# Three groups of small transfers move from SyncE's DMA queue to GpSimd's, in a backbone layer pair with chunked delta-rule heads

## The chip, the cores and the metric

The kernel runs on one core of one Trainium2 chip. The metric is the device time of one execution in microseconds. The engines are named as in the profile: PE (TensorE matmuls), PEld (its weight loads), DVE (VectorE), ACT (ScalarE), POOL (GpSimd) and SP (SyncE, which only issues DMAs here). A DMA can be issued from SP, from ACT or from POOL; each of the three has a queue of its own, and a wait in front of an issue holds everything behind it on that engine.

## The reference

The reference is a two-layer backbone over 256 latent tokens and 256 context tokens, all in float32, with a width of 2048. Layer 0 joins gated delta-rule heads (run in both directions over chunks of 64 tokens) with neighbourhood-attention heads. Layer 1 is a gated short convolution. Each layer has a SwiGLU block of hidden width 5632. The part that the change touches is the delta rule, and in it the inverse of a triangular matrix for each chunk, head and direction:

```python
m = jnp.where(i[:, None] > i[None, :], jnp.einsum('bhnid,bhnjd->bhnij', kb, k) * decay, 0.0)
t_inv = lax.linalg.triangular_solve(eye + m, eye, left_side=True, lower=True, unit_diagonal=True)
u = t_inv @ (v * beta);  w = t_inv @ (kb * exp(gc))
# scan over the chunks, with state S, for each direction
v_new = u_c - w_c @ S
o_c   = qd_c @ S + a_c @ v_new              # latent tokens only
S     = S * exp(gl_c) + kd_c.T @ v_new
```

The scan runs first over the context, from a zero state, and then over the latent tokens from the state that the context leaves. The context gives no output of its own.

## The kernel before, in words

**The main stream.** The time is filled with large matrix products. Weights come from HBM in tiles of 128 x 1024 floats (`raw`, 4 buffers, issued on SP at L235). ACT rounds each to float32r (`whi`, L175) and DVE takes the remainder (`wlo`, L249), with 3 buffers of each. PE then makes three products for each pair of inputs (hi x hi, hi x lo, lo x hi), at L302, L303, L307 and L319 where tokens are the output's partitions, and at L347 where features are. Beside it an adaptive-norm job streams `ada_w` through DVE (`araw`, issued at L435, used at L441).

**The order.** The program is written as generators that are interleaved by hand; a list of steps (`plan`, with the constants `P_CH` and `P_INV`) says at which step of the main stream the delta-rule parts are written. The scheduler of the framework then orders each engine's instructions once, from a simulated timeline and by the program's order as priority. On the chip each engine works through its list in order.

**The delta rule.** It is done for the context (`seq` = 1) and then for the latent tokens (`seq` = 0), in two groups of four heads (`q`).

- `chunk_matrices(seq)` builds the matrices `nt` (L994, DVE) block by block, for 2 x 2 pairs of `q` and token half. Their 32-wide off-diagonal blocks are copied by POOL into `n32` (L1013), the 64-wide ones by ACT into `n64` (L1015), the diagonal blocks into `dgs`. `nt` has one buffer. `n64` and `n32` are stored to HBM (L1020, L1021) and `dgs` too (L1023). The diagonal blocks come back in another layout as `lsol`, are inverted on DVE in 31 steps of forward substitution (L1036, L1038), and the inverses and their transposes are stored as `dz` (L1045: 4 DMAs, two out of `lsol`).
- `load_diag(dz, q)` clears two tiles with POOL, `xd` (L1060) and `xdT` (L1061), and loads the inverses' diagonal blocks into them: 8 DMAs on SP (L1066), each of 32 rows with 16 runs of 128 bytes. It is called four times, so there are 32 such DMAs. `xd` lies in one room (`diag`, or `kT` for the last call); `xdT` has two buffers, so its loads can be issued one call ahead.
- `inverses(off, diag, q)` completes the inverse from blocks of 32 to 64 and to 128, with small matmuls (L1092, L1099, L1105).
- `scan(q, seq, ...)` runs the recurrence with matmuls (L1130, L1139, L1150, L1158, L1172), DVE (L1133, L1163, L1174) and ACT (L1154). It loads keys (`ktok`, L956) and values (`vtok`, L956). For the context's second group the keys lie in the room of `lsol`.
- All of these parts take their PSUM banks from one pool of two (`gd`), in the order of the program: first inverse, second inverse, the two context scans, the latent tokens' two inverses, the two latent scans. The names in the code are `own_chunks`, `first_inverse`, `second_inverse`, `first_own` and `latents`.

**What runs meanwhile on the main stream.** Keys and values of the attention heads (`kb_d`, `vb_d`, staged through `nst`, 3 buffers, copied out of PSUM at L170 and L172 and stored on SP at L1260), then the queries, for which the context's half of the input is dropped and the latent half is loaded again as `hC`, with 7 DMAs of 512 KB on POOL (L1284). Then the attention itself (with `kb`, `vb` and `br` loaded on SP), the gate, and the output projection. The projection takes the attention's features first and the delta rule's (`yhi`, `ylo`) last.

The program reserves a scratch for the descriptors of POOL's DMAs: `dynamic_dma_scratch_size=1024` (L1702), in bytes of each partition.

Of the kernel before, what the change touches and what calls it, by code (L numbers as in the profile page):

```python
# [111 lines left out]
def body(tc, x, c, ctx, c_ctx, ada_w, ada_b, norm_mix, norm_ffn, ffn_w_gate, ffn_w_up, ffn_w_down,  # L112
# [3 lines left out]
    PE, ACT, DVE, POOL, SP = nc.tensor, nc.scalar, nc.vector, nc.gpsimd, nc.sync  # L116
# [43 lines left out]
    def smt():  # L160
        small.append(small.pop(0))
        return small[0].tile([128, 512], F32, name="sm", tag="sm")
# [11 lines left out]
    def acopy(dst, src):  # L174
        ACT.activation(dst, src, AF.Copy)  # L175
# [367 lines left out]
    def gdt():  # L543
        return gdp.tile([128, 512], F32, name="gd", tag="gd")
# [18 lines left out]
    p = smt()  # L563
# [114 lines left out]
    kd = dram.tile([128, 4, 8, 128], F32, name="kd")  # L678
# [5 lines left out]
    def hslice(d_, t0, n, q):  # L684
        return d_[:, t0:t0 + n, q * 4:q * 4 + 4, :].rearrange("p t h e -> p t (h e)")
# [125 lines left out]
    for b in range(8):  # L811
# [4 lines left out]
        p = smt()  # L816
# [119 lines left out]
    def g4(name, tag, bufs=1):  # L936
        return gw.tile([128, 1024], F32, name=name, tag=tag, bufs=bufs)

    def g2(name, bufs=G2):
        return gw.tile([128, 4, 128], F32, name=name, tag="m2", bufs=bufs)  # L940
# [10 lines left out]
        ACT.activation(em, pD.rearrange("p (i e) -> p i e", i=4), AF.Exp)  # L951
        return em

    def load_tok(tag, d_, t0, q, room=None):
        t = (g4(tag, tag) if room is None else room).rearrange("p (t h e) -> p t h e", t=2, h=4)
        SP.dma_start(t.rearrange("p t h e -> p t (h e)"), hslice(d_, t0, 2, q))  # L956
        return t

    def load_feat(tag, src, pool_=None, bufs=1):
        t = (pool_ or gw).tile([128, 1024], F32, name=tag, tag=tag, bufs=bufs).rearrange("p (h t) -> p h t", h=4)  # L960
        SP.dma_start(t, src)
        return t

    def chunk_matrices(seq):


        t0 = 2 * seq
        if seq:
            n64 = gw.tile([128, 16, 64], F32, name="n64", tag="n64", bufs=1)
            n32 = gw.tile([128, 16, 32], F32, name="n32", tag="n32", bufs=1)  # L970
            dgs = g4("dgs", "diag")
        else:
            n64 = lgo.tile([128, 1024], F32, name="n64", tag="o_t", bufs=2).rearrange("p (n c) -> p n c", n=16)
            n32 = g4("n32", "vtok")[:, 0:512].rearrange("p (n c) -> p n c", n=16)
            dgs = lgo.tile([128, 1024], F32, name="dgs", tag="o_t", bufs=2)
        dgs = dgs.rearrange("p (n c) -> p n c", n=32)
        for q in range(2):
            ktok = load_tok("ktok", kd, t0, q)
# [6 lines left out]
            for ti in range(2):  # L985
# [25 lines left out]
                for j in range(4):  # L1011
                    d, i = j % 2, j ^ 1
# [4 lines left out]
        lsol = g4("lsol", "lsol").rearrange("p (r c) -> p r c", r=32)  # L1017
        nd64 = dram.tile([128, 16, 64], F32, name="nd64", tag="nd64", bufs=2)
        nd32 = dram.tile([128, 16, 32], F32, name="nd32", tag="nd32", bufs=2)
        SP.dma_start(nd64, n64)  # L1020
        SP.dma_start(nd32, n32)  # L1021
        dl = dram.tile([4, 32, 32, 32], F32, name="dl", tag="dl", bufs=2)
        SP.dma_start(dl.rearrange("b r n c -> (b r) n c"), dgs)  # L1023
        for b in range(4):
# [16 lines left out]
        dz = dram.tile([2, 4, 2, 2, 8, 1024], F32, name="dz", tag="dz", bufs=2)  # L1041
# [14 lines left out]
    def load_diag(dz, q, tag="diag"):  # L1056

        xd = g4("xd", tag).rearrange("p (n c) -> p n c", n=16)
        xdT = gw.tile([128, 16, 128], F32, name="xdT", tag="xdT", bufs=XDT)
        POOL.memset(xd, 0.0)  # L1060
        POOL.memset(xdT, 0.0)  # L1061
        for b in range(4):
            s_ = slice(b * 32, b * 32 + 32)
            c_ = slice((b % 2) * 32, (b % 2) * 32 + 32)
            for v, m_ in ((0, xd[s_, :, c_]), (1, xdT[s_, :, s_])):
                SP.dma_start(m_, dz[v, b, q].rearrange("d t (r c) -> r (d t) c", r=32))  # L1066
        return xd, xdT

    def inverses(off, diag, q):
# [42 lines left out]
    def scan(q, seq, xdT, AT=None, qT=None, kT=None, o_t=None):  # L1112

        hs = [q * 4 + i for i in range(4)]
        if kT is None:
            kT = load_feat("kT", kTd[:, seq, q * 4:q * 4 + 4, :])
        ktok = load_tok("lsol" if seq and q else "ktok", kd, 2 * seq, q)
        vtok = load_tok("vtok", vd_, 2 * seq, q, lgo.tile([128, 1024], F32, name="vtok1", tag="o_t", bufs=2) if seq and q else None)
        visited = set()
        for step in range(2):  # L1120
            for d in range(2):
                ti = step if d == 0 else 1 - step
                tt = 2 * seq + ti
                tok = slice(ti * 128, ti * 128 + 128)
                zero = seq and step == 0
                sv = state[:, d, q * 4:q * 4 + 4, :]
                if not zero:
                    pP = gdt()
                    for i in range(4):
                        PE.matmul(pP[:, i * 128:(i + 1) * 128], kT[:, i, tok], sv[:, i, :], start=True, stop=True)  # L1130
                    R = g2("R")
                    for i in range(4):
                        DVE.scalar_tensor_tensor(R[:, i, :], pP[:, i * 128:(i + 1) * 128],  # L1133
                                                 negegc[:, d, tt, hs[i]:hs[i] + 1], vtok[:, ti, i, :],
                                                 op0=OP.mult, op1=OP.add)
                if not seq:
                    pQ = gdt()
                    for i in range(4):
                        PE.matmul(pQ[:, i * 128:(i + 1) * 128], qT[:, i, tok], sv[:, i, :], start=True, stop=True)  # L1139
                    for i in range(4):  # L1140
                        o = o_t[:, ti, i, :]
                        e = eg[:, 0, d, tt, hs[i]:hs[i] + 1]
                        if tt in visited:
                            DVE.scalar_tensor_tensor(o, pQ[:, i * 128:(i + 1) * 128], e, o, op0=OP.mult, op1=OP.add)
                        else:
                            ACT.activation(o, pQ[:, i * 128:(i + 1) * 128], AF.Copy, scale=e)
                pY = gdt()
                for i in range(4):
                    rhs = vtok[:, ti, i, :] if zero else R[:, i, :]
                    PE.matmul(pY[:, i * 128:(i + 1) * 128], xdT[:, d * 8 + ti * 4 + i, :], rhs, start=True, stop=True)  # L1150
                if seq or step == 0:
                    vd = g2("vd")
                    for i in range(4):
                        ACT.activation(vd[:, i, :], pY[:, i * 128:(i + 1) * 128], AF.Copy,  # L1154
                                       scale=brest[:, d, tt, hs[i]:hs[i] + 1])
                    pS = gdt()
                    for i in range(4):
                        PE.matmul(pS[:, i * 128:(i + 1) * 128], ktok[:, ti, i, :], vd[:, i, :], start=True, stop=True)  # L1158
                    if zero:
                        acopy(sv, pS.rearrange("p (i e) -> p i e", i=4))  # L1160
                    else:
                        for i in range(4):
                            DVE.scalar_tensor_tensor(sv[:, i, :], sv[:, i, :], eg[:, 2, d, tt, hs[i]:hs[i] + 1],  # L1163
                                                     pS[:, i * 128:(i + 1) * 128], op0=OP.mult, op1=OP.add)
                if not seq:
                    vn = g2("vn")
                    for i in range(4):
                        ACT.activation(vn[:, i, :], pY[:, i * 128:(i + 1) * 128], AF.Copy,
                                       scale=beta[:, d, tt, hs[i]:hs[i] + 1])
                    pA = gdt()  # L1170
                    for i in range(4):
                        PE.matmul(pA[:, i * 128:(i + 1) * 128], AT[:, d * 8 + ti * 4 + i, :], vn[:, i, :], start=True, stop=True)  # L1172
                    ov = o_t[:, ti]
                    DVE.tensor_tensor(ov, ov, pA.rearrange("p (i e) -> p i e", i=4), op=OP.add)  # L1174
                visited.add(tt)

    ATs = []
    parts = chunk_matrices(1)

    for q in range(2):  # L1180
# [40 lines left out]
    def own_chunks():  # L1221
        nonlocal off, diag, own
        own = chunk_matrices(0)
        off = load_offdiag(parts)
        diag = load_diag(parts[2], 0)

    def first_inverse():
        nonlocal diag
        xdTs.append(inverses(off, diag, 0))
        diag = load_diag(parts[2], 1)  # L1230

    def second_inverse():
        nonlocal off, diag
        xdTs.append(inverses(off, diag, 1))
        for q in range(2):
            scan(q, 1, xdTs[q])
        xdTs.clear()
        off = load_offdiag(own)
        diag = [load_diag(own[2], q, ("diag", "kT")[q]) for q in range(2)]
# [176 lines left out]
    def norm_row(t):  # L1416

        DVE.tensor_reduce(ss2[:, t:t + 1], ssx[:, t, :], axis=AX.X, op=OP.add)
        return rstd(rpool, ss2[:, t:t + 1], [128, 1], 1, D, f"nx{t}")
# [222 lines left out]
    for half in range(2):  # L1642
# [8 lines left out]
        for f in range(8):  # L1651
            k = half * 8 + f
            p = smt()
# [25 lines left out]
    for t in range(2):  # L1679
        r = norm_row(t)  # L1680
        for n in range(2):
            for m in range(2):
                v = xs[:, t, (2 * n + m) * 512:(2 * n + m + 1) * 512]
# [34 lines left out]
```

## Time and profile before

| What | Value |
|---|---|
| median of three runs | 2697.98 us (2696.09 to 2699.02) |
| the profiled execution | 2700.74 us |
| its span | 2698.6 us |
| PE busy | 2646.0 us, 98% of the span |
| DVE busy | 1915.9 us, 71% |
| ACT busy | 1274.9 us, 47% |
| POOL busy | 47.8 us, 2% |
| mean DMA rate | 253 GB/s |

The difference of 2.1 us between time and span lies outside the program's own instructions. The delta-rule parts lie between 230 and 785 us of the span; everything after that is feed-forward, the short convolution and their weights. Matmuls overlap in the records (one of 512 columns follows another after 0.227 us, though each is shown with 0.39), so a busy PE is not read as a PE at its peak; an idle one is a stop. In the timelines a row has its start, its length, engine, line and tiles, and in brackets the idle time of the engine before it and what ended that. A group of waits shows the sum, the number and the longest. SPq stands for SP's queue.

### The profile page before, as it was taken

The numbers are of one execution on the slowest core, as the hardware profiler recorded it, in microseconds if no ns is written. First come the engines' busy times: TensorE is split into PE (matmuls) and PEld (weight loads), VectorE is DVE, ScalarE is ACT, GpSimd is POOL, SyncE is SP. The second block draws the span as 40 slices with busy tenths as digits, with TensorE's granted clock in tenths as the row PEclk, the third lists the DMA queues.
The fourth block names the chain that finished last, engine by engine and source line by source line (L and its number), as shares of the span: only waits on it lengthen the run. The fifth ranks groups of instructions, "written<-read, shape, count | busy, mean of one in ns | idle before, by whom it ended". The sixth has DMA issues, their size and how long they took to land.

```text
span 2698.6 us, 37488 instructions
## 1 busy us (share of the span) xinstructions
PE 2646.0 (98%) x13775; PEld 2183.0 (81%) x13775; DVE 1915.9 (71%) x2645; ACT 1274.9 (47%) x1848; POOL 47.8 (2%) x73
## 2 busy tenths in 40 slices
PE   6999999999999999999999999999999999999998
PEld 4688888888887888888888878888788888888886
DVE  3378798866698866776788878898565655545665
ACT  3258633235455444444455564444454444445554
POOL 0000101010000000000000000000000000000000
PEclk8999999999999999999999999999999999999999
DMA  9945588996496988888887859997576777666653
GB/s 368 357 150 172 182 267 262 295 306 188 158 348 239 330 290 293 291 288 291 277 294 261 298 180 331 334 338 255 167 254 220 238 228 237 209 202 212 194 195 110
DMA packets 280027, 682.02 MB, mean 253 GB/s; under 512 B 50813, under 2 KB 93461, under 8 KB 278435
## 3 DMA queue, kind: packets, MB, share of 16 engines
q1 hardware_dynamic: 273516, 666.46, 73.5%
q10 hardware_dynamic: 4423, 9.50, 1.0%
q0 software_dynamic: 1904, 3.67, 0.4%
q8 instruction: 108, 1.77, 0.3%
q14 instruction: 76, 0.62, 0.1%
HBM read 657.48 MB, written 22.05 MB: 252 GB/s over the span
## 4 chain that ended last, share of the span: by engine, by line
PE 90%; DVE 3%; DMA 3%; ACT 1%; SPq 1%; issue 1%; DVEq 0%; ACTq 0%
PE mm L302 21%; PE mm L307 21%; PE mm L303 21%; PE mm L347 10%; PE mm L319 8%; PE sm L194 2%; PE sm L605 1%; PE gd L347 1%; DMA araw<-in_ada_w_dram 1%; DMA dz<-lsol 1%; DVE acc L441 1%; PE sm L1328 0%; PE gd L949 0%; DMA xn<-in_ctx_dram 0%; DVE wlo L249 0%
## 5 line engine op out<-in xcount | busy, mean ns | idle before, releaser
L249 DVE TENSOR_TENSOR wlo<-raw,whi 128x1024 fp32r<-128x1024 f32 x800 | 971.9, 1222 | 458.6 <-ACT whi L175 450.0
L175 ACT ACTIVATE whi<-raw 128x1024 fp32r<-128x1024 f32 x800 | 843.9, 1062 | 844.1 <-PE mm L307 627.8
L302 PE MATMUL mm<-whi,fhi 128*128 128x512 f32 x1232 | 482.0, 393 | 2.6 <-DVE fhi L1475 2.6
L303 PE MATMUL mm<-wlo,fhi 128*128 128x512 f32 x1232 | 479.7, 390 | 0.5 <-DVE wlo L249 0.5
L307 PE MATMUL mm<-whi,flo 128*128 128x512 f32 x1232 | 389.9, 390 | 0.0
L407 DVE SCALAR_TENSOR_TENSOR acc<-araw,cT,acc 128x1024 f32<-128x1024 f32 x224 | 286.7, 1280 | 39.8 <-DMA araw<-in_ada_w_dram 36.9
L302 PEld LDWEIGHTS mm<-whi,fhi 128*128 128x128 f32 x1232 | 231.3, 188 | 50.9 <-DVE fhi L1475 4.0
L307 PEld LDWEIGHTS mm<-whi,flo 128*128 128x128 f32 x1232 | 231.1, 188 | 48.4
L303 PEld LDWEIGHTS mm<-wlo,fhi 128*128 128x128 f32 x1232 | 231.2, 188 | 47.7 <-DVE wlo L249 1.2
L302 PE MATMUL mm<-whi,ahi 128*128 128x512 f32 x664 | 259.0, 390 | 0.0
L303 PE MATMUL mm<-wlo,ahi 128*128 128x512 f32 x664 | 258.3, 389 | 0.0
L347 PE MATMUL mm<-hB,whi 128*128 128x512 f32 (+1 forms) x840 | 234.6, 366 | 1.0 <-DVE hB L629 1.0
L307 PE MATMUL mm<-whi,alo 128*128 128x512 f32 x664 | 206.6, 389 | 0.0
L347 PEld LDWEIGHTS mm<-hB,whi 128*128 128x128 f32 x840 | 147.7, 189 | 24.5 <-DVE hB L629 2.3
L178 ACT ACTIVATE ahi<-prodT 128x256 fp32r<-128x256 f32 x176 | 73.0, 418 | 182.9 <-PE mm L303 178.0
L347 PE MATMUL mm<-hB,wlo 128*128 128x512 f32 (+1 forms) x420 | 149.7, 365 | 0.0
L307 PEld LDWEIGHTS mm<-whi,alo 128*128 128x128 f32 x664 | 124.6, 188 | 26.0
L302 PEld LDWEIGHTS mm<-whi,ahi 128*128 128x128 f32 x664 | 124.7, 188 | 25.7
L303 PEld LDWEIGHTS mm<-wlo,ahi 128*128 128x128 f32 x664 | 124.6, 188 | 25.6
L441 DVE SCALAR_TENSOR_TENSOR acc<-araw,cT,acc 128x512 f32<-128x512 f32 x180 | 133.9, 746 | 2.9 <-DMA araw<-in_ada_w_dram 2.3
L302 PE MATMUL mm<-whi,dhi 128*128 128x512 f32 x336 | 131.1, 392 | 1.2 <-DVE dhi L1475 1.2
L303 PE MATMUL mm<-wlo,dhi 128*128 128x512 f32 x336 | 130.7, 390 | 0.0
(412 smaller groups left out, 3523.3 us busy)
## 6 DMA issues: line engine op xcount, KB each, us to landing
araw<-in_ada_w_dram SPq DMA_DIRECT2D x288, 512.0 KB, 5.3
raw<-in_ffn_w_down_dram SPq DMA_DIRECT2D x176, 512.0 KB, 4.7
raw<-in_ffn_w_gate_dram SPq DMA_DIRECT2D x160, 512.0 KB, 4.4
raw<-in_ffn_w_up_dram SPq DMA_DIRECT2D x160, 512.0 KB, 4.7
raw<-in_ev_w_in_dram SPq DMA_DIRECT2D x112, 512.0 KB, 4.2
araw<-in_ada_w_dram SPq DMA_DIRECT2D x192, 256.0 KB, 5.1
raw<-in_od_w_in_dram SPq DMA_DIRECT2D x96, 512.0 KB, 5.1
raw<-in_ev_w_out_dram SPq DMA_DIRECT2D x32, 512.0 KB, 7.0
```

The lines of the kernel that those rows point to most:

```text
L175: ACT.activation(dst, src, AF.Copy)
L178: ACT.activation(hi, src, AF.Copy)
L194: return PE.transpose(dst, src, ident[:n, :n])
L249: last_lo[0] = DVE.tensor_tensor(lo, raw, hi, op=OP.subtract).ins
L302: PE.matmul(ps[ti][n], a, hi[:, n * 512:(n + 1) * 512], start=first, stop=False)
L303: ins = PE.matmul(ps[ti][n], a, lo[:, n * 512:(n + 1) * 512], start=False, stop=False).ins
L307: last_mm[0] = PE.matmul(ps[ti][n], b, hi[:, n * 512:(n + 1) * 512], start=False, stop=False).ins
L319: ins = PE.matmul(ps[ti][n], a(t), w[:, c_], start=False, stop=a is ll and hi is group[-1][0]).ins
L347: last_mm[0] = PE.matmul(o, wt, h_(slice(0, len(ws)), mv, k), start=i == 0 and g == 0 and j == 0, stop=i == len(ks) - 1 and g == len(group ...
L407: DVE.scalar_tensor_tensor(acc, raw, cT[:, k:k + 1], acc, op0=OP.mult, op1=OP.add)
L441: DVE.scalar_tensor_tensor(accs[n], raws.pop(i), cT[:, k:k + 1], accs[n], op0=OP.mult, op1=OP.add)
L605: ins = PE.matmul(pr[32 * j:32 * j + 32, :], cT2[:, g + j, :], raw[:, j].rearrange("p s n -> p (s n)"), start=g == 0, stop=g == KT - 4).ins
```

## The change

Three groups of DMAs are issued from POOL instead of SP: the store of `n32` (L1021, 2 DMAs of 256 KB), the loads of the inverse's diagonal blocks (L1066, 32 DMAs of 64 KB), and the load of the context's second keys (the call of `load_tok` in `scan` with `seq` and `q` both 1, 1 DMA of 512 KB). Nothing is added or taken away; sizes, sources, targets and tiles stay as they are.

```diff
-    def load_tok(tag, d_, t0, q, room=None):
+    def load_tok(tag, d_, t0, q, room=None, queue=SP):
         t = (g4(tag, tag) if room is None else room).rearrange("p (t h e) -> p t h e", t=2, h=4)
-        SP.dma_start(t.rearrange("p t h e -> p t (h e)"), hslice(d_, t0, 2, q))
+        queue.dma_start(t.rearrange("p t h e -> p t (h e)"), hslice(d_, t0, 2, q))
         return t
...
         SP.dma_start(nd64, n64)
-        SP.dma_start(nd32, n32)
+        POOL.dma_start(nd32, n32)
...
             for v, m_ in ((0, xd[s_, :, c_]), (1, xdT[s_, :, s_])):
-                SP.dma_start(m_, dz[v, b, q].rearrange("d t (r c) -> r (d t) c", r=32))
+                POOL.dma_start(m_, dz[v, b, q].rearrange("d t (r c) -> r (d t) c", r=32))
...
-        ktok = load_tok("lsol" if seq and q else "ktok", kd, 2 * seq, q)
+        ktok = load_tok("lsol", kd, 2 * seq, q, queue=POOL) if seq and q else load_tok("ktok", kd, 2 * seq, q)
```

## The prediction

> **What bounds the kernel now.** I read the page first, then PE's waits in the stretch that the edit touches (380 to 780 us), then the windows around the one long wait, and last the queue of SP and the timelines of POOL, DVE and ACT there.
>
> ```profile
> span 2698.6 us, 37488 instructions
> ...
> PE 2646.0 (98%) x13775; PEld 2183.0 (81%) x13775; DVE 1915.9 (71%) x2645; ACT 1274.9 (47%) x1848; POOL 47.8 (2%) x73
> ...
> PE 90%; DVE 3%; DMA 3%; ACT 1%; SPq 1%; issue 1%; DVEq 0%; ACTq 0%
> ```
>
> PE is the bound. A DMA that leaves SP earlier is worth only the PE time that is now lost waiting. PE's waits from 380 to 780 us:
>
> ```profile
> PE mm L347 <- DVE nst L172: 3.4, 1, 3.4
> PE gd L1130 <- DMA kT<-kTd: 1.0, 1, 1.0
> PE mm L347 <- issue: 0.6, 1, 0.6
> ```
>
> So 5.0 us of visible idle, most of it one wait. The windows from there on (PE's busy time and matmuls first, granted clock, DMA share and GB/s last):
>
> ```profile
> 564.00:568.00 4.00, 0.63 (x5) 0.63 (x6) 1.35 (x2) 0.71 (x3) 1.39 (x1) 1.00 0.72 200
> 568.00:572.00 4.00, 4.00 (x24) 4.00 (x23) 3.01 (x4) 2.11 (x2) 0.00 (x0) 0.57 0.98 250
> 572.00:576.00 4.00, 4.00 (x36) 4.00 (x36) 2.65 (x7) 2.09 (x5) 0.00 (x0) 1.00 1.03 375
> ```
>
> The wait costs more than its idle: in the 4 us after it the granted clock is 0.57 and PE runs 24 matmuls, where the next 4 us have 36. That is 4 x (1 - 24/36) = 1.3 us by count and 4 x 0.43 = 1.7 by clock; I take 1.5. The wait is worth 3.4 + 1.5 = 4.9 us. Where does it come from? From SP's queue, whose own waits between 380 and 700 us include:
>
> ```profile
> SPq L956 <- DMA dz<-lsol: 8.9, 1, 8.9
> ...
> SPq L1021 <- POOL n L1013: 5.9, 1, 5.9
> ...
> SPq L1020 <- ACT n L175: 0.8, 1, 0.8
> ```
>
> ```profile
> 547.64 0.33 SPq L435 DMA_DIRECT2D araw<-in_ada_w_dram  x1
> 557.00 0.38 SPq L956 DMA_DIRECT2D lsol<-kd  x1
> ...
> 561.15 3.62 SPq L1260 DMA_DIRECT2D vb_d<-nst  x3
> ```
>
> ```profile
> 552.96 0.69 DVE L172 COPY nst<-mm 128x512 f32<-128x512 f32 x1 [1.59 <-PE mm L319]
> ...
> 566.62 0.69 DVE L172 COPY nst<-mm 128x512 f32<-128x512 f32 x1 [6.10 <-DMA vb_d<-nst]
> ```
>
> The load of the second keys (L956, into the room lsol) waits until the stores of dz have read lsol, and SP is in order: from 548.0 to 557.0 nothing leaves it. Behind it stand the stores of the values. The last source that DVE wrote was begun at 552.96, yet they leave from 561.15 on. So the next copy into nst finds no free buffer until 566.62, the PSUM bank stays taken, and PE stops.
>
> **The change, part by part.**
>
> *The second keys' load, 1 DMA of 512 KB, L956 to POOL.* SP no longer stands from 548.0 to 557.0. With the dz loads gone too, the value stores follow when their data is there, about 555 instead of 561.15. They land 4.2 us after issue, about 559, before DVE asks for the buffer at 566.62 - 6.10 = 560.5. Gain 4.9 us of PE. On POOL the load stands in the same wait, behind the last hC load and ahead of the memset of xdT that POOL then waits to do, so nothing new is late. PE reads it first at 577.01:
>
> ```profile
> 577.01 1.06 PE L1158 MATMUL gd<-vd,lsol 128*128 128x128 f32 x8
> ```
>
> ```profile
> vb_d<-nst SPq DMA_DIRECT2D x8, 256.0 KB, 4.2
> ```
>
> *The store of n32, 2 DMAs of 256 KB, to POOL.* It stands behind the copies that fill n32 on the same engine, so it waits for nothing. SP's 5.9 us go, but the store of n64 is next on SP and left only 1.2 us after it, released by ACT's copy of n64 (the wait of 0.8 above). SP would stand there instead.
>
> ```profile
> 471.24 0.33 SPq L1021 DMA_DIRECT2D nd<-n  x1
> 472.46 0.33 SPq L1020 DMA_DIRECT2D nd<-n  x1
> ```
>
> PE lost nothing there before. I cost it at 0, between -1.2 and 0.
>
> *The 32 loads of the diagonal blocks, 64 KB each, to POOL.* SP's own 0.3 to 0.5 us per issue were hidden. The price lies on POOL:
>
> ```profile
> 501.28 0.96 POOL L1060 MEMSET xd<- 128x1024 f32 x1 [23.23 <-PE gd L1092]
> ...
> 529.28 2.26 POOL L1284 DMA_DIRECT2D hC<-h_d  x3 [2.21 <-PE mm L307]
> 538.73 0.72 POOL L1284 DMA_DIRECT2D hC<-h_d  x1 [7.19 <-issue]
> 541.44 1.36 POOL L1284 DMA_DIRECT2D hC<-h_d  x1 [1.98 <-issue]
> ...
> 593.17 0.95 POOL L1060 MEMSET xd<- 128x1024 f32 x1 [27.79 <-DMA raw<-in_ev_w_in_dram]
> 599.43 1.82 POOL L1061 MEMSET xdT<- 128x2048 f32 x1 [5.31 <-PE gd L1150]
> ```
>
> ```profile
> DMA to landing us min/median/max: 7.8/10.1/13.0
> ```
>
> ```profile
> q0 software_dynamic: 1904, 3.67, 0.4%
> ```
>
> ```profile
> xdT<-dz SPq DMA_DIRECT2D x16, 64.0 KB, 2.9
> xd<-dz SPq DMA_DIRECT2D x16, 64.0 KB, 3.0
> ```
>
> The seven hC loads are all that this queue (q0) does before. Three leave at once, in 2.26 us; the fourth only 9.45 us after the first, about as long as one takes to land (the landing row is that of hC). So the queue takes a limited number of packets: three loads of 1904 / 7 = 272 are in, 816, and a fourth, 1088, is not. A dz load is 512 runs of 128 bytes (32 rows of 16), with 16 more by hC's count 528; two are 1056. The trace decides only that the limit is from 816 to below 1088; 1056 is nearest the upper end, so I take one dz load at a time. (The Trainium skill, "DMA: Bandwidth & Descriptors", section Terms, gives a descriptor 16 bytes, and the kernel reserves 1024 bytes a partition: by that, an estimate, 64 for each of 16 engines, and two loads with 33 each don't fit. The rows of hC agree with it: 51 in, 68 not.)
>
> One at a time, a load costs its landing and the restart of the queue. I call it C. SP's dz loads land 3.0 us after issue; 9.45 minus the first hC's landing is unknown but small, I take 0.3: C = 3.3 us. Bounds: two at a time gives 1.65; hC's least landing, 7.8, is the far end, with eight times the bytes. The nearest row is dz's own, hence 3.3.
>
> Where it matters is the second inverse, whose four xd loads can start only after the memset at 501.28:
>
> ```profile
> 504.93 2.35 SPq L1066 DMA_DIRECT2D xd<-dz  x4
> ```
>
> ```profile
> 511.60 0.74 PE L1092 MATMUL gd<-xd,n 32*32 32x32 f32 x62
> ```
>
> Before, they left SP by 507.3, landed about 510.3, and PE read them from 511.60. On POOL the first leaves at 502.3, and the last lands at 502.3 + 4 x 3.3 = 515.5: 3.9 us after PE's reading. (C at 1.65: 508.9, no delay; at 7.8: 533.5, 22 us.) From there the inverses, the scans and the latents follow each other through the two gd banks up to the output projection, whose last four inner blocks read what the last latents give:
>
> ```profile
> 783.55 1.28 DVE L179 TENSOR_TENSOR ylo<-sm,yhi 128x512 fp32r<-128x512 f32 x2
> ```
>
> ```profile
> 792.17 2.72 PE mm L319 x12
> ...
> 891.89 5.44 PE mm L319 x24
> ```
>
> The last two blocks start about 792.17; the two ahead of them are 24 matmuls, 5.44 us, so the group starts about 786.7. Its data is complete at 784.83: room 1.9 us. The chain of scans ran through the stop at 564 too and wins its 4.9 us as PE does, so it arrives 4.9 - 3.9 = 1.0 us earlier, and PE, 4.9 us earlier, waits for it: the end moves by -1.0 - 1.9 = -2.9 us. The other three batches have cover: the last one starts at 594.1, and eight loads with a memset of 1.8 us between land at 594.1 + 1.8 + 26.4 = 622.3, before PE reads the last of them:
>
> ```profile
> 625.99 0.72 PE L1099 MATMUL gd<-xdT,Y 32*32 32x32 f32 x62
> ```
>
> If that cover is gone it costs 8C - 30.1 us. The first batch, 12 loads from 415.5, takes 12C = 39.6 us on POOL, to 455, and the copies into n32 may stand behind them:
>
> ```profile
> 415.46 0.86 SPq L1066 DMA_DIRECT2D xdT<-dz  x2
> ...
> 421.74 2.61 SPq L1066 DMA_DIRECT2D xdT<-dz  x5
> ```
>
> ```profile
> 452.21 2.15 DVE L994 SCALAR_TENSOR_TENSOR nt<-gd,beta,em 128x128 f32<-128x128 f32 x8
> ```
>
> DVE's writing at 452.21 must find the copies of the block before done: if they stood behind all twelve, DVE would be some 4 us late, which the three split weight buffers of 24 matmuls each (16 us) hide. Cost 0.
>
> **Sum.** The profiled execution took 2700.74 us, 2.1 us outside the span, and is 2.8 us above the median of 2697.98. -4.9 for the stop, +2.0 given back at the output projection, 0 elsewhere: -2.9. On the profiled time 2697.8; on the median 2695.1. The scheduler also orders all engines anew around the moved issues, a scatter of a few us that no row prices.
>
> **Rivals.**
> *The whole stop is won* (faster, 0.29). The loads overlap, C is at or below 2.5, so 4C ends by 512.3 and the chain keeps its 4.9 us. The kT wait of 1.0 us goes too, because that load no longer queues with dz loads: -5.9, 2692.1. For it: dz's landing on SP is 2.9 with a full queue ahead of it. Against: the hC rows.
>
> *POOL's one-at-a-time loads set the chain* (slower, 0.22). The place is the second inverse and the last batch. The delay is 4C - 9.3 and 8C - 30.1, less 4.9 and 1.9. At C = 4.2 that is 7.5 + 3.5 - 6.8 = 4.2, at 4.3 it is 5.4: from there it is slower by over 0.2%. At C = 5 it is 10.7 + 9.9 - 6.8 = 13.8, 2711.8. For it: DMA share 0.98 in the window from 568 us, and hC's 512 KB, sharing the engines, need 7.8 at least. Against: dz has an eighth of the bytes. The Trainium skill, "SBUF — State Buffer", in its warning on DVE blocking DMAs from GpSimd, says that a DVE copy in a two-port mode keeps GpSimd from writing descriptors. By that C would grow with DVE's load; hC's issues of 0.72 and once 1.36 us would allow 0.6 us, C = 3.9 and still no loss of 0.2%.
>
> *The copies into n32 hold DVE* (slower, 0.06). At C = 5 the twelve loads end at 475.5, DVE stands 24 us at its next block and the 16 us of split weights run out: +8 - 2.9, about 2703.1. It decides from C = 4.5 on, if the copies come behind all twelve.
>
> **How the numbers follow.** What a measurement of this kernel can tell from no change is about 0.2%, 5.4 us. My own forecast, part of the stop won and part given back, has 0.43, from -5.4 to +5.4. So faster 0.29, same 0.43, slower 0.28. The time is that of the likeliest, 2695.1. The range goes down to 2689 (the full gain, with 3 us of scatter) and up to 2712 (C about 5), leaving some 0.1 on each side; the likeliest alone spans 2692.6 to 2703.4.
>
> **What would show it.** Right: no wait of PE on nst near 564 and no clock of 0.57 after it; the value stores follow their copies within some 3 us; q0 has 1904 + 32 x 528 + 272 + 2 x 144 = 19360 packets; on POOL, successive xd loads stand 3 to 4 us apart; the second inverse reads xd near 515. A PE wait on the latents' features at the output projection shows what was given back. Wrong: dz loads under 2 us apart (the first rival), or over 4.3 us apart with PE waiting on xd, xdT or at the projection (the second), or DVE standing at nt with POOL behind dz loads (the third).

## The result, and the profile after

| | before | after |
|---|---|---|
| median | 2698.31 us (4 runs, 2696.09 to 2699.02) | 2735.11 us (4 runs, 2733.88 to 2736.12) |
| span of the profiled execution | 2698.6 us | 2732.9 us |

The ratio is 1.0142, with a 95% interval of 1.0130 to 1.0154: the change costs 36.8 us. The forecast was 2695.1 us with a range to 2712; the time lies outside it. The page of the kernel after, its first lines and the shares of the chain that ended last:

```profile
span 2732.9 us, 37516 instructions
...
PE 2649.5 (97%) x13775; PEld 2186.7 (80%) x13775; DVE 1915.0 (70%) x2645; ACT 1275.0 (47%) x1848; POOL 70.8 (3%) x108
...
PE 90%; issue 4%; DMA 2%; DVE 1%; ACT 1%; POOL 1%; SPq 1%; ACTq 0%; POOLq 0%; DVEq 0%
```

PE's busy time is the same within 3.5 us, so the loss is idle time and clock. The share of "issue", time in which an engine waited for nothing that the profile shows, has gone from 1% to 4%. PE's waits between 200 and 900 us of the kernel after (sum, number, longest):

```profile
PE gd L194 <- DVE nt L994: 23.3, 1, 23.3
PE gd L1099 <- DMA xdT<-dz: 7.4, 2, 5.6
PE gd L1092 <- DMA xd<-dz: 4.6, 2, 2.5
...
PE mm L347 <- DVE nst L172: 1.1, 1, 1.1
```

The last row is the stop that the change was to remove: 3.4 us before, 1.1 now. The three above it are new. The first leads from PE to DVE and from there to POOL. DVE's timeline at that place:

```profile
427.31 0.75 DVE L441 SCALAR_TENSOR_TENSOR acc<-araw,cT,acc 128x512 f32<-128x512 f32 x1
452.02 2.16 DVE L994 SCALAR_TENSOR_TENSOR nt<-gd,beta,em 128x128 f32<-128x128 f32 x8 [23.97 <-POOL n L1013]
```

And POOL's, from its first load of `dz` on:

```profile
411.16 0.68 POOL L1066 DMA_DIRECT2D xdT<-dz  x1 [0.78 <-DMA dz<-lsol]
417.14 0.66 POOL L1066 DMA_DIRECT2D xdT<-dz  x1 [5.30 <-issue]
419.73 0.65 POOL L1066 DMA_DIRECT2D xdT<-dz  x1 [1.93 <-issue]
...
450.02 0.66 POOL L1066 DMA_DIRECT2D xd<-dz  x1 [1.87 <-issue]
450.72 1.27 POOL L1013 COPY n<-nt 32x128 f32<-32x128 f32 x4
```

Twelve loads leave one by one between 411.16 and 450.02. Only then does POOL copy the *first* block of `nt` into `n32`, which DVE had written at 412.44. In the kernel before, POOL's first copy of that inverse came 1.2 us after DVE's writing at 417.3:

```profile
418.50 0.61 POOL L1013 COPY n<-nt 32x128 f32<-32x128 f32 x2 [3.28 <-DVE nt L994]
```

`nt` has one buffer, so DVE cannot write the second block until 452.02. DVE works through its list in order, and behind the waiting instruction stand the splits of the weights (`wlo`); ACT waits 30.0 us with its copy of the same block into `n64`, with its roundings behind it. PE stops about 3 us after DVE, but not for want of weights. Its next instruction, a transpose of keys (L194), writes into a `gd` bank, and the wait ends when DVE's second block, which reads `gd`, has been written. Behind it in PE's list stand 19 matmuls of a weight tile that is already split: PE runs them from 455.0 us on, while DVE's next split begins only at 459.11.

To see where the 36.8 us arise, take ACT's 800 roundings of weight tiles (`whi`), which come in the same order in every version. The table gives how much later one starts in the kernel after than in the kernel before, less the same difference at 300 us (-3.5 us; the profiled execution of before had a slower beginning). Each value is the mean of six neighbouring tiles.

| place (us of before) | 480 | 510 | 555 | 575 | 600 | 640 | 660 | 1000 | 2500 |
|---|---|---|---|---|---|---|---|---|---|
| later by, us | 25.1 | 28.1 | 30.2 | 27.7 | 28.5 | 35.7 | 37.7 | 37.3 | 37.7 |

So 25 us are lost at the first block, 5 at the second inverse's waits for `xd`, 2.5 come back where the stop near 564 was, and 9 to 10 are lost at the last batch's waits for `xdT`. Behind 660 nothing more is lost. The windows of the kernel after show how much of each is clock (PE's busy time first, the granted clock, DMA share and GB/s last):

```profile
431.00:454.00 23.00, 0.00 (x0) 0.00 (x0) 1.98 (x8) 0.42 (x1) 6.30 (x13) 0.54 0.12 37
454.00:460.00 6.00, 5.76 (x16) 4.71 (x17) 5.93 (x12) 3.67 (x8) 1.64 (x2) 0.50 0.51 161
460.00:464.00 4.00, 4.00 (x29) 3.60 (x28) 3.96 (x7) 1.80 (x3) 0.00 (x0) 0.96 0.82 246
...
655.00:660.00 5.00, 0.91 (x76) 0.92 (x78) 0.00 (x0) 0.00 (x0) 0.65 (x1) 0.50 0.23 58
660.00:664.00 4.00, 4.00 (x90) 3.94 (x77) 2.37 (x5) 1.50 (x4) 0.00 (x0) 0.50 0.01 4
```

A granted clock of half lasts 27.3 us at the first stop, but some 21 of them fall into the stop itself and cost nothing; the 6 us after it, at 0.50, cost about 3. At the last batch about as long a stretch at 0.50 follows the stop, again some 3 us beside the 7.4 of waiting.

### The profile page after: what moved, and what is told of

It reads as the page before. It is cut to its first block, busy times and chain, and to the rows that moved or that the text cites. A ratio compares the mean times of both kernels' runs of the same rounds, so it can differ in the third digit from the quotient of the medians.

```text
span 2732.9 us, 37516 instructions
## 1 busy us (share of the span) xinstructions
PE 2649.5 (97%) x13775; PEld 2186.7 (80%) x13775; DVE 1915.0 (70%) x2645; ACT 1275.0 (47%) x1848; POOL 70.8 (3%) x108
## 2 busy tenths in 40 slices
DMA packets 263899, 682.02 MB, mean 250 GB/s; under 512 B 34429, under 2 KB 77077, under 8 KB 262307
## 4 chain that ended last, share of the span: by engine, by line
PE 90%; issue 4%; DMA 2%; DVE 1%; ACT 1%; POOL 1%; SPq 1%; ACTq 0%; POOLq 0%; DVEq 0%
PE mm L302 21%; PE mm L307 21%; PE mm L303 21%; PE mm L347 10%; PE mm L319 8%; PE sm L194 2%; PE sm L605 1%; PE gd L347 1%; DMA araw<-in_ada_w_dram 0%; PE gd L949 0%; PE sm L1352 0%; DMA cs<-in_cst_dram 0%; PE gd L1150 0%; PE mm L194 0%; POOL xdT L1066 0%
```

## Experiments

The ratios are those on record; they need not be the quotient of the two medians. The theory: on POOL only one load of `dz` is under way at a time, because POOL's queue holds a limited number of runs; the order of POOL's list puts all twelve loads of the first batch ahead of the first copies into `n32`, and DVE waits for those. The rivals: the transfers themselves are slow there; or another part of the change pays.

| run | median us | before us | ratio, 95% interval |
|---|---|---|---|
| e1_keys_store | 2704.06 | 2698.80 | 1.0013 (1.0004 to 1.0023) |
| e2_diag_only | 2730.02 | 2698.80 | 1.0106 (1.0092 to 1.0121) |
| e3_ab5 | 2744.36 | 2698.80 | 1.0161 (1.0145 to 1.0178) |
| e4_ab5_ring2048 | 2707.19 | 2698.80 | 1.0023 (1.0010 to 1.0036) |
| e5_copies_act | 2715.36 | 2696.91 | 1.0062 (1.0044 to 1.0080) |
| e6_first_sp | 2711.89 | 2696.91 | 1.0064 (1.0047 to 1.0081) |
| e7_halves | 2692.76 | 2696.91 | 0.9988 (0.9979 to 0.9997) |
| e8_diag_act | 2709.83 | 2696.91 | 1.0048 (1.0033 to 1.0063) |
| e9_keys_only | 2696.87 | 2697.48 | 0.9995 (0.9986 to 1.0004) |
| e10_store_only | 2703.93 | 2697.48 | 1.0025 (1.0015 to 1.0034) |
| e11_halves_diag | 2701.13 | 2697.48 | 1.0008 (0.9999 to 1.0017) |
| e12_quarters | 2701.51 | 2697.48 | 1.0016 (1.0007 to 1.0024) |
| e13_halves_keys | 2697.24 | 2697.88 | 1.0000 (0.9992 to 1.0009) |

**Which part pays: e1 and e2.** e1 is the kernel after with the loads of `dz` back on SP, e2 the kernel before with only those on POOL.

```diff
 e1, against after
-                POOL.dma_start(m_, dz[v, b, q].rearrange("d t (r c) -> r (d t) c", r=32))
+                SP.dma_start(m_, dz[v, b, q].rearrange("d t (r c) -> r (d t) c", r=32))
 e2, against before: the opposite edit
```

> Undoes the diagonal blocks' part alone: those 32 loads are back on SP, the second keys and the n32 store stay on POOL. Theory (POOL takes the diagonal loads one at a time, with the n32 copies behind twelve of them, and DVE and PE stop for it): the copies follow DVE's writing within 1 us again, PE's stop of 23 us and its waits on xd and xdT are gone, and SP's 9 us wait in front of the second keys too, so 2693 to 2698 us. Rival (the second keys or the store on POOL cost by themselves, behind or between the hC loads): 2705 us or more, with a PE wait on hC, lsol or n32.

> The diagonal blocks' part alone on POOL; second keys and n32 store on SP as before. Theory: the stop of 23 us is there in full, and so are the waits on xd and xdT; SP's wait in front of the second keys is back: 2730 to 2742 us. Rival (the three parts hurt only together, by filling POOL's queue): 2700 to 2715 us.

e2 alone costs 31.2 us, and PE's waits between 200 and 900 us begin with the same three rows as after:

```profile
PE gd L194 <- DVE nt L994: 20.3, 1, 20.3
PE gd L1099 <- DMA xdT<-dz: 4.3, 1, 4.3
PE gd L1092 <- DMA xd<-dz: 4.1, 2, 3.1
```

In e1 none of the three is longer than 1.6 us. The loads of `dz` are the cause. e1 also missed its expectation: it should have gained a few us and lost 5; that is taken up with e9 and e10.

**Slow transfers, or a full queue: e3 and e4.** Doubling the scratch for descriptors needs room in SBUF, so both kernels have one buffer of `AB` less; between them only the scratch differs, and the lists of ACT, DVE, POOL and SP are the same instruction by instruction (PE's too, but for 18 of 13775 rows, small matmuls of L1099 and L1105 that run beside each other and are recorded in another order).

```diff
 e3 and e4, against after
-AB = 6
-AHEAD = 6
+AB = 5
+AHEAD = 5
 e4 only
-    nc = _bacc.Bacc("TRN2", target_bir_lowering=False, num_devices=1, dynamic_dma_scratch_size=1024)
+    nc = _bacc.Bacc("TRN2", target_bir_lowering=False, num_devices=1, dynamic_dma_scratch_size=2048)
```

> A control for the next: the changed kernel with one buffer less for the adaptive-norm weights (5 instead of 6), which frees 2 KB of each partition. Nothing else. If the buffer hardly matters: 2731 to 2740 us, with the stop of 23 us.

> The control with twice the scratch for the descriptors of POOL's DMAs (2048 bytes of each partition for 1024), the order of POOL's instructions being the same. Theory (the scratch holds 64 descriptors for each DMA engine, a diagonal load takes 33, so only one is in flight): with 128 three are in flight, the twelve loads leave in 12 to 20 us instead of 39, DVE's stop falls from 24 to 0 to 5 us, PE's to 0 to 3, and the hC loads leave seven at once: 2698 to 2708 us. Rival (the transfers themselves are slow on this queue, since they share the DMA engines with the weights in small runs): the loads still leave 3 to 5 us apart and it stays at 2725 us or more.

POOL's timeline in e3, with 1024 bytes:

```profile
410.58 0.68 POOL L1066 DMA_DIRECT2D xdT<-dz  x1 [0.77 <-DMA dz<-lsol]
416.74 0.66 POOL L1066 DMA_DIRECT2D xdT<-dz  x1 [5.48 <-issue]
419.27 0.65 POOL L1066 DMA_DIRECT2D xdT<-dz  x1 [1.87 <-issue]
```

In e4, with 2048:

```profile
410.58 1.96 POOL L1066 DMA_DIRECT2D xdT<-dz  x3 [0.81 <-DMA dz<-lsol]
417.06 1.94 POOL L1066 DMA_DIRECT2D xdT<-dz  x3 [4.53 <-issue]
...
428.50 0.66 POOL L1066 DMA_DIRECT2D xd<-dz  x1 [2.64 <-issue]
429.20 1.27 POOL L1013 COPY n<-nt 32x128 f32<-32x128 f32 x4
```

Three leave at once instead of one, the last of the twelve leaves 18 us after the first instead of 37, PE's wait for `nt` falls from 22.3 to 3.5 us, and no wait of PE for a load of `dz` is left. The loads of `hC` change with it: in e3 three leave at once, in e4 all seven.

```profile
532.52 4.92 POOL L1284 DMA_DIRECT2D hC<-h_d  x7 [7.13 <-PE mm L307]
```

e4 is 37.2 us faster than e3 with the same work in the same order. That the scratch limits what is under way is shown, and slow transfers as the main cause fall. Both kernels wait 5.3 us for `rtmp` (near 885 in e3, 847 in e4), which after does not; e3 is 9.3 us slower than after and 4.4 above what was expected of it, and where the rest of that is lost was not followed.

**Smaller pieces: e7 and e12.** If the limit counts the runs under way, cutting each load lets more of it be in flight, with the scratch unchanged.

```diff
 e7, against after (e12: four pieces of 4 blocks each)
-                POOL.dma_start(m_, dz[v, b, q].rearrange("d t (r c) -> r (d t) c", r=32))
+                src = dz[v, b, q].rearrange("d t (r c) -> r d t c", r=32)
+                for d in range(2):
+                    POOL.dma_start(m_[:, d * 8:d * 8 + 8, :], src[:, d])
```

> After's kernel with each load of dz (512 runs of 128 bytes) cut into two of 256 runs: the same bytes and runs, twice as many instructions. Theory (GpSimd's queue holds a fixed number of runs under way, so one whole load or three halves): three halves are under way at a time, the next leaves before the one ahead has landed, and the spacing for a whole load falls from 3.5 us to 2 to 3 us; the stop of 23.3 us shrinks to 5 to 12 us; 2,708 to 2,722. The other theory (one instruction at a time, whatever its size): twice as many landings of at least 2.2 us one after another, spacing 4.4 us or more for a whole load, the stop grows to 35 us or more and the time is 2,742 or above.

> After's kernel with each load of dz in four DMAs of 128 runs, 128 in all. Theory (a fixed number of runs under way): six or seven quarters are under way at a time and landings no longer space them; what spaces them is GpSimd's issue, about 0.6 us each or 2.4 us for a whole load, a little less than in e7_halves: 2,689 to 2,696. The other theory (GpSimd's own time per issue is now the limit, 128 x 0.6 = 77 us, and copies stand behind it): a wait of 3 us or more for nt or xd comes back, 2,697 to 2,708.

POOL's timeline in e7:

```profile
409.70 1.75 POOL L1068 DMA_DIRECT2D xdT<-dz  x3
416.10 1.74 POOL L1068 DMA_DIRECT2D xdT<-dz  x3 [4.64 <-issue]
...
425.53 0.58 POOL L1068 DMA_DIRECT2D xd<-dz  x1 [0.25 <-issue]
426.15 3.42 POOL L1013 COPY n<-nt 32x128 f32<-32x128 f32 x4
```

And in e12:

```profile
409.94 3.81 POOL L1069 DMA_DIRECT2D xdT<-dz  x7
415.79 3.44 POOL L1069 DMA_DIRECT2D xdT<-dz  x6 [2.04 <-DMA xdT<-dz]
```

One whole load, three halves, seven quarters leave before the queue stands. With 33, 17 and 9 units a piece on each of 16 engines that is 33, 51 and 63, and one piece more would be 66, 68 and 72; three whole loads with the doubled scratch are 99, a fourth would make 132. All four lie on the two sides of 64 units for 1024 bytes, and of 128 for 2048. The loads of `hC` fit as well: with 272 packets each, 17 for an engine, three are 51 and four 68, and the seven that leave at once in e4 are 119. (The Trainium skill, "DMA: Bandwidth & Descriptors", section Terms, gives a descriptor 16 bytes, so 64 in 1024; the counts agree with it. That the limit holds for each engine and that a piece has one unit beside its data are read from these counts.)

e7 went further than its theory said. Its list also has the first four copies after 14 halves instead of after all 24, so DVE never waits for them, and between 400 and 800 us PE's longest wait is this:

```profile
PE gd L949 <- DVE nt L994: 1.7, 1, 1.7
```

Its median is 4.2 us below that of before (0.12% by the ratio); each against the kernel before that was measured beside it, it is 41 us faster than the kernel after. By the same measure as above it runs 1.0 us late at 510, 5.4 us early at 575, and 3.9 early at the end: the stop near 564 is won. e12 has its seven in flight but loses 4 us against before; the new waits are neither at `nt` nor at `xd`, as its second theory had it, but 6.3 us for `o_t` at 776, where the lists stand in another order, and 2.0 us for `nst` at 555 (below).

**The link through the copies: e5 and e6.** e5 puts the copies into `n32` on ACT and leaves the loads where they are; e6 puts the eight loads that are called first on SP and leaves four of the first twelve.

```diff
 e5, against after
-                    POOL.tensor_copy(n32[j * 32:j * 32 + 32, n0:n0 + 4, :], nt[...])
+                    acopy(n32[j * 32:j * 32 + 32, n0:n0 + 4, :], nt[...])
 e6, against after (load_diag has an argument queue=POOL)
-        diag = load_diag(parts[2], 0)
+        diag = load_diag(parts[2], 0, queue=SP)
```

> After's kernel with the sixteen copies into n32 (per inverse) moved from GpSimd to ScalarE; the 32 loads of dz stay on GpSimd, one at a time. Theory (the copies of the first block, queued behind the twelve loads, are the link between GpSimd's loads and VectorE's second nt): the stop of TensorE at 23.3 us and most of its 27.3 us of half clock go, and what stays are the waits for xd and xdT (7.4 + 4.6 us in after) with the half clock near 539 and 655; 2,703 to 2,714. The other theory (what hurts is the order and traffic of the loads themselves, the copies only stand beside them): the twelve loads still take about 40 us, so the time stays at 2,725 or above and another wait of about 20 us stands near 430 to 455. If the copies hold ScalarE's queue instead, small stops at ScalarE's rows appear and the end is 3 to 6 us above the theory's.

> After's kernel with the one call of eight loads that GpSimd issues first of the twelve on SP's queue; four stay at the head of GpSimd's queue. Theory (GpSimd's copies wait for as many loads as stand before them, about 3.5 us each): the copies into n32 leave about 4 x 3.5 = 14 us after the first load, not 40; the stop of TensorE falls from 23.3 us to 0 to 4 us, its half clock with it; the later loads still cost up to 12 us of waits for xd and xdT; 2,703 to 2,717. The other theory (any load of dz on GpSimd at that place stops the chain, whatever the number): the stop stays above 15 us and the time at 2,722 or above.

In e5 the loads still leave one by one, from 417.36, yet no wait of PE for `nt` is longer than 1.1 us; from 400 to 800 us its longest is this:

```profile
PE gd L1092 <- DMA xd<-dz: 5.2, 2, 2.7
```

In e6 the copies leave behind four loads:

```profile
411.33 0.68 POOL L1066 DMA_DIRECT2D xdT<-dz  x1 [0.77 <-DMA dz<-lsol]
...
426.97 0.66 POOL L1066 DMA_DIRECT2D xdT<-dz  x1 [4.10 <-issue]
427.67 2.17 POOL L1013 COPY n<-nt 32x128 f32<-32x128 f32 x4
```

That is 16 us after the first load, as 4 x 3.5 = 14 had it roughly, and DVE's second block starts at 429.9, 17 us after the first as it did in before. So the big stop needs both: loads one at a time, and the copies behind twelve of them. What is left, 15 to 18 us above before, holds the waits for `xd` and `xdT` (4.8 and 4.6 us in e6) with their clock; how much of the remainder is the new order of the lists was not separated. e5's median is 1.4 us above what was expected, and its profiled execution took 2706.2 us, 9 us less than the median, so that its rows do not show all that is left.

**Another queue: e8.** The loads of `dz` on ACT.

```diff
-                POOL.dma_start(m_, dz[v, b, q].rearrange("d t (r c) -> r (d t) c", r=32))
+                ACT.dma_start(m_, dz[v, b, q].rearrange("d t (r c) -> r (d t) c", r=32))
```

> After's kernel with the loads of dz on ScalarE's queue; the second keys and the store of nd32 stay on GpSimd. Theory (the loss is that of GpSimd's software queue, not of leaving SP): no copies into n32 wait for loads, the stop of 23.3 us and its half clock are gone, SP is as free as in after, and only ScalarE's work is behind its own issues (32 x about 0.7 us in all, most of it idle time); 2,693 to 2,708. The other theory (loads off SP land late because of traffic, whatever the queue): waits for xd and xdT of 10 us or more stay, 2,715 or above.

The big stop is gone and no wait for `xdT` is left; `xd` waits 0.4 us. But the time is 2 us above the theory's range: PE now waits 3.8 us for `vd` and 1.9 us for `nst`, both written by ACT, and 3.4 us for DVE at L1107. ACT's queue is in order too, and work for PE stands behind its issues or in a new order; which of the two was not separated.

**The other two parts: e9, e10, e11, e13.**

```diff
 e9, against before: only  load_tok("lsol", kd, 2 * seq, q, queue=POOL)
 e10, against before: only  POOL.dma_start(nd32, n32)
 e11, against before: only the two halves of e7
 e13, against e7:  SP.dma_start(nd32, n32)
```

> Before's kernel with only the second keys on GpSimd; dz and nd32 stay on SP. In e1_keys_store, which had the store too, the stop of TensorE near 564 was gone (3.4 us and 1.5 us of half clock), but TensorE stood 3.9 us at 751 and 759 for whi and 2.1 us at 584 for vd, and the time was 2704.1 us. Theory (the second keys' earlier load reorders what follows it, and that costs more than the stop; the store has no part): the stop is gone and the time is as in e1, 2,700 to 2,706. The other theory (the store on GpSimd is what was paid for in e1): 2,692 to 2,696, and no wait of 2 us for whi near 751.

> Before's kernel with only the store of nd32 on GpSimd. The step of the prediction that costs it at nothing: 2,695 to 2,700, with the stop of 3.4 us near 564 and its half clock as in before. The other theory (the store gives away what the keys gain in e1_keys_store): 2,701 to 2,706.

> Before's kernel with only the loads of dz on GpSimd, each in two DMAs of 256 runs; the second keys and the store stay on SP. Theory (with three halves under way at a time GpSimd's copies do not wait, and without dz SP reaches the second keys' load in time): neither the stop of 20 to 23 us nor the one near 564, 2,690 to 2,696, as e7_halves has it. The other theory (the second keys must leave SP too): the stop of 3.4 us near 564 stays, 2,696 to 2,700.

> e7_halves with the store of nd32 back on SP; the second keys and the halves of dz stay on GpSimd. In e10_store_only the store alone cost 6.5 us, lost where ScalarE's newly ordered list reaches whi late at 753 and 761. Theory (that is the order's, not the store's own price): taking the store back gives nothing like 6 us here, since e7_halves has no such wait; 2,690 to 2,698. The other theory (a store on GpSimd's queue costs some 6 us wherever it stands): 2,684 to 2,688.

e9 is the cleanest of all, since its lists of PE, ACT and DVE are those of before. It gains nothing that can be told from zero, which neither of its theories had, because the stop stays (2.4 us and 3.4 us of half clock near 562). SP's queue in e9 shows why:

```profile
543.05 0.33 SPq L435 DMA_DIRECT2D araw<-in_ada_w_dram  x1
551.97 0.86 SPq L1066 DMA_DIRECT2D xd<-dz  x2
...
555.27 1.65 SPq L1260 DMA_DIRECT2D vb_d<-nst  x3
```

Without the keys' load, the loads of `dz` behind it wait for the same stores, from 543.4 to 552.0. The value stores leave 6.8 us after DVE's copy at 548.50, where it was 8.2 us before. e11, with only `dz` off SP, has the mirror image: the second keys leave at 552.96, the third value store right behind at 553.42, and a stop of 1.1 us stays. Its median, 3.7 us above that of before, is outside both of its expectations, though its interval still holds 1. SP is free at this place when both have left it, as in after, e7, e12 and e13, where the first value store leaves within 0.8 us of DVE's copy. That alone doesn't remove the stop: the stores are then slow to land. In e13 SP issues them from 547.50, and DVE's timeline has

```profile
547.27 0.69 DVE L172 COPY nst<-mm 128x512 f32<-128x512 f32 x1 [2.47 <-PE mm L319]
...
557.09 0.69 DVE L172 COPY nst<-mm 128x512 f32<-128x512 f32 x1 [4.64 <-DMA vb_d<-nst]
```

so the buffer comes back 9.6 us after the first issue, and PE stands 2.2 us. In e12 SP issues them from 545.00, and the buffer comes back after 9.5 us; PE stands 2.0 us:

```profile
554.52 0.69 DVE L172 COPY nst<-mm 128x512 f32<-128x512 f32 x1 [9.37 <-DMA vb_d<-nst]
```

Of the four only e7 has no stop; there the copies stand at 548.95 and 556.07, and DVE doesn't wait for a store. Nor must SP be free for the stop to go. In e10 SP stands 7.3 us in front of the second keys and the value stores leave from 560.74, and e1, whose lists of PE, ACT and DVE are those of e10, has SP standing in front of the loads of `dz`; yet PE has no wait for `nst` in either. DVE's copies stand there at 556.60 and 565.80 (e10), with 1.7 us of waiting for a store. So the stop depends on the order of the lists as much as on SP.

e10 costs 6.5 us for two DMAs, although the stop that it was expected to keep is gone. PE's waits from 400 to 800 us begin with rows that before does not have:

```profile
PE mm L302 <- ACT whi L175: 3.9, 2, 2.6
PE gd L1092 <- DMA xd<-dz: 2.1, 1, 2.1
PE gd L194 <- DVE nt L994: 1.7, 1, 1.7
```

The first lies at 753 and 761, 280 us after the store left at 470; the second at 511; the third at 434, before the store left, so the store itself can't have caused it. The lists of ACT, PE and DVE differ from those of before. If the store had a price of its own on POOL, e7 should have gained some 6 us when it went back to SP; e13 went from 4.2 us better than before to 0.6. So no price of the store itself is seen, and the order that the scheduler made is the cause that fits all three; a run with the store on POOL and the old order was not made, so this is argued and not shown. It fits e1's miss too: with the lists of e10, e1 has the same 3.9 us for `whi` (at 751 and 759) and 1.6 us for `nt`, and beside them 2.1 us for `vd` and 1.1 us for `xd`.

## Why the prediction was wrong

**The step that failed** is the first batch of twelve loads, costed at 0. The prediction had its length nearly right (12C = 39.6 us; measured 38.9 from the first to the last issue, and 42 with the last landing), and said that the copies into `n32` might stand behind them. But it asked only whether the *third* block's writing at 452.21 would find them done. POOL's new list has the first block's copies behind all twelve, so it is the second block's writing that stands, about 17 us after the first. The delay is then 39 - 17 = 22 us instead of 4 (DVE stood 24). The cover of 16 us, three split weight buffers, did not count either: PE stopped about 3 us after DVE did, with split weights still in hand, since its own list had reached an instruction whose `gd` bank the waiting block had to free first (L194). Matmuls behind that one could not start, split or not. Measured: 23.3 us of stop and 3 us of clock, 25 us by the lag.

**The rival named for this** (the copies into `n32` hold DVE, 0.06) was the right mechanism. Its price was too low, 8 us instead of 25, and so was its condition: it was tied to C = 4.5 or more, while with the copies of the first block behind the batch DVE is late as soon as 12C exceeds the 17 us between the two blocks, by this estimate from C = 1.5 on.

**C.** One load at a time was right (e3 and e4, and the timeline above). The three rows of `hC` alone had left it open, since two loads, 1056, lay inside their bounds; choosing against two was a guess that held. The restart of 0.3 us was right as well: in the kernel after, a load leaves 0.3 us after the one ahead has landed. The landing, taken from SP as 3.0 us, is what varied (`xd` first, then `xdT`):

```profile
DMA to landing us min/median/max: 2.2/4.1/6.1
DMA to landing us min/median/max: 2.2/3.3/6.4
```

3.3 us nearly holds for the first batch, 39 / 11 = 3.5. Later it does not. The waits of POOL between 380 and 700 us in the kernel after:

```profile
POOL xdT L1066 <- issue: 48.2, 14, 6.0
...
POOL xd L1066 <- issue: 41.8, 13, 5.3
```

90 us of waiting and 0.65 us of issue for each of 27 loads give 4.0 us on average, and from 523 to 626 us successive loads of a batch stand 3.7 to 6.4 us apart. The second rival's place was right as well: PE waits 4.6 us for `xd` at the second inverse and 7.4 us for `xdT` in the last batch. With C = 5 it had 10.7 and 9.9 us late; the lag shows 5 and 9 to 10.

**What was right.** SP did stand behind the second keys, and behind the loads of `dz` once the keys were gone (e9): "with the dz loads gone too" was needed for SP to be free there. The stop near 564 fell from 3.4 to 1.1 us with the change, and to nothing in e7, whose gain of 4.2 us answers to the 4.9 that were forecast. That it came so near is partly luck: in e12 and e13 SP is as free and the stop stays, in e1 and e10 SP stands and the stop is gone, so e7's order had a part in it. What stays of the stop after the change is the landing of the value stores, taken as 4.2 us. SP issues them in the kernel after at

```profile
580.82 3.06 SPq L1260 DMA_DIRECT2D vb_d<-nst  x3
```

and DVE gets the buffer back 9.3 us later:

```profile
590.09 0.69 DVE L172 COPY nst<-mm 128x512 f32<-128x512 f32 x1 [7.82 <-DMA vb_d<-nst]
```

What was to be given back at the output projection can't be seen in the kernel after, which arrives there late: its lag does not change between 660 and 1000 us. e7 arrives early, and PE doesn't wait for `yhi` or `ylo`. It gives back 1.3 us near 845 us of before for another reason: both kernels have a wait of 2.45 us for `acc` there, and the granted clock is at 0.50 beside it for 3.4 us in before and for 6.8 us in e7.

**The store at 0.** As a transfer nothing speaks against it (e7 and e13); in effect it was wrong when alone (e10, +6.5 us). The prediction spoke of a scatter of a few us by the new order of the lists and put no size on it in its range; e10 and e12 show 4 to 6.5 us of it.

**The packets.** Forecast for q0 were 19360; the page of the kernel after has

```profile
DMA packets 263899, 682.02 MB, mean 250 GB/s; under 512 B 34429, under 2 KB 77077, under 8 KB 262307
...
q0 software_dynamic: 3232, 6.82, 0.8%
```

The reading that a load fills the queue by its 512 runs was right, but the runs don't travel as packets there (below).

## What to carry to other kernels

Before a DMA moves to another engine's queue, write out that engine's list as it will be and ask for each instruction behind the issues who waits for it. An issue is cheap only while the queue has room: count the runs of each transfer against what the queue was seen to hold, and where they do not fit, cut the transfer or enlarge the scratch (here 36.8 us slower became 4.2 us faster by cutting each load in two). When a wait is removed from an in-order queue, look at what stands next in it with the same dependence, and try the pieces in pairs as well as alone; a few us of difference may be no more than the new order of the lists.

## What the runs showed of the hardware

- The same 32 transfers need far fewer packets on POOL's queue than on SP's. Packets under 512 bytes fall from 50813 to 34429, that is by 16384 = 32 x 512, one for each run of 128 bytes. With only these loads moved (e2), q0 has 2928 packets, 1024 more than before: 32 for each load. 64 KB over 16 engines is 4 KB each, so one packet of data and one small one per engine fits; cut into halves (64 loads) there are 512 more under 512 bytes, in quarters 1537, as that count asks (512 and 1536). The queue's room is nevertheless taken by the runs, as e7 and e12 show.
- When POOL's queue has no room, POOL itself stands, and its copies and memsets with it, though the profile mostly names no releaser ("issue"). In before this showed only between loads of `hC`, where nothing stood behind.
- A granted clock of 0.50 outlasts a stop of PE. Around the stop of 23.3 us (from 431 us) it begins 2 us after the stop does and ends some 6 us after work resumes (433 to 460 us); around the stop of 5.6 us (from 653.5) it lasts from 654.9 to 665.1, again 6 us into the work. These two cost about the same in clock, some 3 us. In before, the stop of 3.4 us near 564 is over when the clock falls, at 568.4, for 3.4 us. The length is not fixed by the stop: the wait of 2.45 us for `acc` has 3.4 us at 0.50 in before and 6.8 us in e7. (The Trainium skill, "TensorE: Matmul & The Clock Gate", Part 1, has a free-running window of 3.4 us by which the clock falls and rises; the stretches in this trace, 27.3, 6.8 and 10.2 us, are multiples of it.)
